# A two-layer encoder on one core: masks added by the row-maximum operation, the rotation's second stage a unit later, turns in three pieces of heads

## The chip, the cores and the metric

The kernel runs on one core of a Trainium2 chip. The metric is device time in microseconds (us) of one execution of the whole program; lower is better. The core's engines are PE (TensorE: matrix products and transposes), DVE (VectorE), ACT (ScalarE), POOL (GpSimd) and SP, which here issues DMAs. Each engine executes its own instructions strictly in the order in which they stand, and waits for others through semaphores. Matrix products write to PSUM banks, everything else lies in SBUF.

## The reference

Two groups of rows, a prompt of 256 and a sample of 512, go through two layers of width D = 1024. Each sub-layer is `x + post_norm(f(pre_norm(x)))`. Layer 0 mixes by windowed attention with sinks, layer 1 by differential attention; each is followed by a SwiGLU layer. Cut to the two mixers:

```python
# layer 0: 16 query heads of 64, 4 key/value heads, window 128
sc = jnp.where(valid, sc, -jnp.inf)                  # |q - k| <= 128, inside the sequence
m = jnp.maximum(jnp.max(sc, axis=-1, keepdims=True), sink)
e = jnp.exp(sc - m)
p = e / (jnp.sum(e, axis=-1, keepdims=True) + jnp.exp(sink - m))

# layer 1: 8 heads, each with two query/key parts of 64 and values of 128
q, k = apply_rope(q, cos, sin), apply_rope(k, cos, sin)
#   apply_rope: [x1 * c - x2 * s, x2 * c + x1 * s]
p = jax.nn.softmax(sc, axis=-1)
a = p[:, :, 0] - lam * p[:, :, 1]
o = rms_norm(a @ v, subln_g) * (1.0 - lambda_init)   # per head
```

## The kernel before

The 768 rows are six tiles of 128: tiles 0 and 1 the prompt, 2 to 5 the sample. Matrix products with weights are made in fp32 precision from three products of high and low parts, high x high, high x low, low x high (`product_steps`, L346 to L348). A tile framework places the instructions: the program's text gives the order in which they are issued, and each engine keeps its share of it, shifted only where the framework's scheduler sees an operand late.

**First mixer** (some 20 to 262 us of the trace). 24 units of 4 key/value heads x 6 tiles; each unit has four items, one for each query head. `score` makes an item's scores (sc, 128 x 256 or 128 x 384, L661 and L662), `normalize` divides by the sum, `turn_e` transposes the block (tpe, L697) for the value products (poa). `item(n)` puts in a row the scores of item n, the normalising of item n - 1 and the turn of item n - 3, and between the items stand the products with weights of a later unit (pqa), shared out evenly by `weave`. The mask of the window is added on PE: two constant bf16 blocks (`mask_l`, `mask_r`) are multiplied by a bf16 identity into the same PSUM bank (L664, L666), 64 times each. DVE then takes the row maximum (L668) and scales it against the sink (negm, L671); ACT makes the exponential out of PSUM with its sum (L677) and the sink's exponential (L679); DVE adds, inverts and scales (L686 to L688).

**Second mixer** (some 790 to 1115 us). The products with weights come in 50 units (`b_fill`): 32 for q and k by head and half of the rows (`rotated`), 18 for v. At the end of a q or k unit, `end` rotates: ACT copies the product out of PSUM (xq, xk), four DMAs on POOL's queue write a copy with the partitions swapped (L836), DVE multiplies x by the cosine (z, L838) and the swapped copy by the sine (L839), adds (L840), ACT casts the high part (qb, kb, L849), DVE subtracts for the low part (L852, L856). Scores and values of the attention (`score`, `turn_e`, `values`: bsc, be, tpa, aT, pob) are placed between the products by a table `events` of times in units; `placed` puts each at its fraction of its unit. Head h, tile t is score number 6h + t. After the 50 units a list `run` written by hand orders the rest (the tail): scores and values of the last heads, turns of the attention's output (tp_o, hhi, L438 and L445), and the first products with the output weights (po). `values` normalises groups of heads, 0 to 3, 4 to 6 and 7, with a reciprocal root that POOL computes (L390, L391) and multiplies in (L944). The turn of a tile is made in two pieces, heads 0 to 3 and 4 to 7.

The lines of the table of times, before:

```python
for h, start, stop in (
        (0, 12, 16.7), (1, 16.7, 22.2), (2, 22.2, 28.8), (3, 29.6, 34.8), (4, 34.8, 40.3), (5, 40.3, 46)):
    spread(h, start, stop)
events += [(47.9 + t / 2, "s", 6 * NT + t) for t in range(4)]
```

## Time and profile before

| | |
|---|---|
| time, median of 3 runs (smallest, largest) | 1678.19 us (1677.85, 1679.21) |
| the profiled execution: its own time, its span | 1678.24 us, 1676.5 us |
| busy: PE, DVE, ACT, POOL | 98%, 74%, 56%, 10% of the span |
| TensorE's clock granted in 140 to 180 us | 1.00 |

The profiled execution is as long as the median, so durations from its trace can be set against the runs without a correction. Times in the profile are microseconds from the span's start; a row of the timeline gives start, duration, engine, line, operation, tile written and tiles read, and in brackets how long the engine had been idle and what ended it. A group's row gives busy time in all and the mean of one in nanoseconds, then the idle time ahead of its instructions and what ended it. PE's products overlap, so what one costs is the distance to the start of the next. Line numbers are those of the kernel before; most of the same statements stand three lines higher after the change.

### The profile page before, as it was taken

What the parts mean: (1) busy time and instruction counts of PE and PEld (TensorE: products, weight loads), DVE (VectorE), ACT (ScalarE), POOL (GpSimd) and SP (SyncE); (2) the same over time, 40 slices, a digit from 0 to 9 for tenths busy, and PEclk for the clock granted to TensorE, in tenths of its full rate; (3) what the DMA queues carried; (4) which work ended last, traced back from release to release, by engine and by line L of the source; (5) the groups of instructions that cost most, each with busy time, mean ns of one, the idle gap of its engine ahead of it and who ended that gap; (6) DMA issues with size and microseconds to landing.
All of it is one profiled execution on the core that took longest, in us unless ns stands there. A gap on an engine that the chain in (4) does not pass through costs nothing. (4 is left out here: it accounts for less than half of the span.)

```text
span 1676.5 us, 25190 instructions
## 1 busy us (share of the span) xinstructions
PE 1638.5 (98%) x9291; PEld 1495.1 (89%) x9291; DVE 1235.2 (74%) x2210; ACT 943.9 (56%) x2080; POOL 162.5 (10%) x276
## 2 busy tenths in 40 slices
PE   7999999999999999999999999999899999999998
PEld 7888878899999998888999989877899999998886
DVE  7888776896766656988685775765897666666985
ACT  6777775654444444556566666675744444444653
POOL 1000001000000000001330451331000000000000
PEclk9999999999999999999999999999999999999999
DMA  5111014534233337675432322314434343337664
GB/s 214 39 39 47 15 39 148 179 131 143 101 127 108 129 125 246 225 268 192 127 84 61 76 71 75 104 31 139 166 119 147 104 142 109 129 115 242 237 244 156
DMA packets 68187, 217.53 MB, mean 130 GB/s; under 512 B 9248, under 2 KB 13472, under 8 KB 67808
## 3 DMA queue, kind: packets, MB, share of 16 engines
q1 hardware_dynamic: 54576, 175.93, 30.9%
q0 software_dynamic: 13344, 39.73, 8.1%
q8 instruction: 73, 1.20, 0.3%
q14 instruction: 50, 0.41, 0.1%
q10 hardware_dynamic: 144, 0.26, 0.0%
HBM read 163.59 MB, written 42.86 MB: 123 GB/s over the span
## 5 line engine op out<-in xcount | busy, mean ns | idle before, releaser
L254 DVE TENSOR_TENSOR wlo<-wraw,whi 128x1024 fp32r<-128x1024 f32 (+2 forms) x174 | 204.6, 1179 | 176.7 <-ACT whi L253 175.2
L253 ACT CAST whi<-wraw 128x1024 fp32r<-128x1024 f32 (+2 forms) x174 | 175.8, 1012 | 119.9 <-PE py L347 59.1
L346 PE MATMUL py<-hhi,whi 128*128 128x384 f32 x464 | 155.4, 335 | 0.9 <-ACT u L1029 0.9
L348 PE MATMUL py<-hhi,wlo 128*128 128x384 f32 x464 | 155.0, 334 | 0.0
L347 PE MATMUL py<-hlo,whi 128*128 128x384 f32 x464 | 155.0, 334 | 0.0
L334 ACT CAST hhi<-araw 128x768 fp32r<-128x768 f32 (+1 forms) x74 | 57.6, 783 | 88.7 <-DMA araw<-act 85.9
L348 PE MATMUL pv<-whi,hlo 128*128 128x512 f32 (+1 forms) x240 | 92.2, 384 | 0.4 <-DVE hlo L335 0.4
L346 PE MATMUL pv<-whi,hhi 128*128 128x512 f32 (+1 forms) x240 | 92.4, 385 | 0.0
L347 PE MATMUL pv<-wlo,hhi 128*128 128x512 f32 (+1 forms) x240 | 92.2, 384 | 0.0
L335 DVE TENSOR_TENSOR hlo<-araw,hhi 128x768 fp32r<-128x768 f32 (+1 forms) x74 | 65.3, 890 | 32.3 <-ACT hhi L334 32.2
L346 PEld LDWEIGHTS py<-hhi,whi 128*128 128x128 f32 x464 | 87.1, 188 | 1.8 <-ACT u L1029 1.5
L347 PEld LDWEIGHTS py<-hlo,whi 128*128 128x128 f32 x464 | 87.1, 188 | 0.0
L348 PEld LDWEIGHTS py<-hhi,wlo 128*128 128x128 f32 x464 | 87.1, 188 | 0.0
L346 PE MATMUL po<-whi,hhi 128*128 128x512 f32 x192 | 78.8, 410 | 3.3 <-ACT hhi L445 2.9
L1082 POOL DMA_DIRECT2D act<-st x22 | 19.4, 882 | 635.9 <-DVE st L1081 635.9
L347 PE MATMUL po<-wlo,hhi 128*128 128x512 f32 x192 | 75.4, 393 | 0.8 <-DVE wlo L254 0.8
L348 PE MATMUL po<-whi,hlo 128*128 128x512 f32 x192 | 76.0, 396 | 0.2 <-DVE hlo L335 0.2
L346 PE MATMUL pqa<-whi,hhi 128*128 128x384 f32 x192 | 73.7, 384 | 0.0
L346 PE MATMUL px<-hhi,whi 128*128 128x384 f32 x208 | 70.2, 339 | 2.7 <-ACT hhi L334 2.7
L898 ACT ACTIVATE be<-bsc,bmx 128x512 f32<-128x512 f32 (+1 forms) x96 | 58.5, 614 | 24.6 <-DVE bmx L896 24.3
L347 PE MATMUL px<-hlo,whi 128*128 128x384 f32 x208 | 70.0, 337 | 1.2 <-DVE hlo L335 1.2
L391 POOL TENSOR_TENSOR rstd_post<-rstd_post,mhalf 128x1 f32<-128x1 f32 x23 | 16.4, 716 | 557.9 <-ACT rstd_post L390 557.9
(315 smaller groups left out, 5112.9 us busy)
## 6 DMA issues: line engine op xcount, KB each, us to landing
act<-st POOLq DMA_DIRECT2D x22, 1344.0 KB, 6.6
wraw<-in_wgu SPq DMA_DIRECT2D x56, 512.0 KB, 4.6
araw<-act SPq DMA_DIRECT2D x70, 384.0 KB, 4.1
y_wraw<-in_wgu SPq DMA_DIRECT2D x40, 512.0 KB, 3.8
wraw<-in_wd SPq DMA_DIRECT2D x40, 512.0 KB, 4.0
xd<-x SPq DMA_DIRECT2D x18, 512.0 KB, 3.0
x<-xd SPq DMA_DIRECT2D x18, 512.0 KB, 3.9
wraw<-in_wo SPq DMA_DIRECT2D x16, 512.0 KB, 3.5
```

Source lines behind the costliest of these rows:

```text
L253: state["raw_hi"] = nc.scalar.copy(out=hi, in_=src)
L254: state["raw_lo"] = nc.vector.tensor_tensor(out=lo, in0=src, in1=hi.bitcast(F32), op=ALU.subtract)
L334: state["hi"] = nc.scalar.copy(out=hi, in_=src)
L335: state["lo"] = nc.vector.tensor_tensor(out=lo, in0=src, in1=hi.bitcast(F32), op=ALU.subtract)
L346: nc.tensor.matmul(out, ah, bh, start=start and i == 0, stop=False, skip_group_check=more)
L347: nc.tensor.matmul(out, ah, bl, start=False, stop=False, skip_group_check=more)
L348: nc.tensor.matmul(out, al, bh, start=False, stop=stop and i == last, skip_group_check=more)
L391: nc.gpsimd.tensor_tensor(out=r[:, :w], in0=r[:, :w], in1=mhalf[:, :w], op=ALU.pow)
L898: nc.scalar.activation(out=e[:, :n * P], in_=s, func=AF.Exp, bias=mx, accum_out=den[:, c:c + 1])
L1082: nc.gpsimd.dma_start(out=at_hand[c // 4][:, :, c // 2 % 2], in_=out.pop(c // 2))
```

## The change

First mixer: the two mask blocks become one fp32 block of 384 columns (left, zeros, right), in a pool that is closed after this mixer. One DVE instruction (`tensor_tensor_reduce`) adds the mask to the scores, multiplies by -1/8, writes the result to SBUF and takes its minimum with the negated sink into negm. The exponential reads that result with a scale of -1. Normalising goes by pairs of heads: every second item normalises the two before it, and the sink's exponential is made there for both.

Second mixer: `end` now stops after the multiplication by the cosine; the rest (`rest`: sine, sum, high and low parts, k's DMAs) is issued after the following unit, behind the instruction in `state["mark"]`. The table's times move by 0.2 to 0.8 units, the sixth head has three scores in it in place of four, and a new kind "o" turns heads 0 to 3 of tiles 0 to 2 at units 48.3 to 49.3. Turns come in three pieces (heads 0 to 3, 4 to 6, 7; `turn_heads`), and the hand-written tail is ordered anew with them.

```diff
+    mask = early.tile([P, 3 * P], F32, name="mask")
+    nc.gpsimd.memset(mask, 0.0)
+    for at, step, mult in ((0, 1, -1), (2 * P, -1, 1)):
         nc.gpsimd.affine_select(
-            out=m, in_=m, compare_op=ALU.is_ge, fill=MASK, base=0,
+            out=mask[:, at:at + P], in_=mask[:, at:at + P], compare_op=ALU.is_ge, fill=MASK, base=0,
             pattern=[[step, P]], channel_multiplier=mult,
...
-                left, right = k0 < t, k1 > t + 1
                 nc.tensor.matmul(s, q[i][:, j], kh[gi, first][:, keys], start=True, stop=False)
-                nc.tensor.matmul(s, q[i][:, j], kl[gi, first][:, keys], start=False, stop=not (left or right))
-                if left:
-                    nc.tensor.matmul(s[:, :P], ident_b, masks[0], start=False, stop=not right)
-                if right:
-                    nc.tensor.matmul(s[:, (nk - 1) * P:], ident_b, masks[1], start=False, stop=True)
-                mx = small.tile([P, 1], F32, tag="mx", name=f"mx{i}_{j}")
-                nc.vector.tensor_reduce(out=mx, in_=s, axis=AX.X, op=ALU.max)
+                nc.tensor.matmul(s, q[i][:, j], kl[gi, first][:, keys], start=False, stop=True)
                 h = gi * 4 + j
-                negm = small.tile([P, 1], F32, tag="negm", name=f"negm{i}_{j}")
-                nc.vector.tensor_scalar(
-                    out=negm, in0=mx, scalar1=-HD ** -0.5, scalar2=nsink[:, h:h + 1], op0=ALU.mult, op1=ALU.min)
                 if j % 2 == 0:
-                    e2[0] = new_y(f"e{i}_{j}")
-                e = e2[0][:, j % 2 * 512:j % 2 * 512 + nk * P]
-                den = small.tile([P, 2], F32, tag="den", name=f"den{i}_{j}")
-                nc.scalar.activation(
-                    out=e, in_=s, func=AF.Exp, bias=negm, scale=HD ** -0.5, accum_out=den[:, 0:1])
-                nc.scalar.activation(out=den[:, 1:2], in_=negm, func=AF.Exp, bias=sink[:, h:h + 1])
-                blocks[i, j] = e, den
-
-            e2 = {}
+                    pair[0] = (
+                        new_y(f"e{i}_{j}"), small.tile([P, 2], F32, tag="negm", name=f"negm{i}_{j}"),
+                        small.tile([P, 4], F32, tag="den", name=f"den{i}_{j}"))
+                e2, negm, den = pair[0]
+                e, c = e2[:, j % 2 * 512:j % 2 * 512 + nk * P], slice(j % 2, j % 2 + 1)
+                side = (k0 - t + 1) * P
+                nc.vector.tensor_tensor_reduce(
+                    out=e, in0=s, in1=mask[:, side:side + nk * P], scale=-HD ** -0.5, scalar=nsink[:, h:h + 1],
+                    op0=ALU.add, op1=ALU.min, accum_out=negm[:, c])
+                nc.scalar.activation(out=e, in_=e, func=AF.Exp, bias=negm[:, c], scale=-1.0, accum_out=den[:, c])
+                blocks[i, j] = e, den, negm
+
+            pair = {}
 
             def normalize(i, j):
-                e, den = blocks[i, j]
-                nc.vector.tensor_tensor(out=den[:, 0:1], in0=den[:, 0:1], in1=den[:, 1:2], op=ALU.add)
-                nc.vector.reciprocal(out=den[:, 0:1], in_=den[:, 0:1])
-                nc.vector.tensor_scalar(out=e, in0=e, scalar1=den[:, 0:1], scalar2=None, op0=ALU.mult)
+                h = (i // NT) * 4 + j
+                _, den, negm = blocks[i, j]
+                nc.vector.tensor_tensor(out=den[:, 2:4], in0=negm, in1=sink[:, h:h + 2], op=ALU.add)
+                nc.scalar.activation(out=den[:, 2:4], in_=den[:, 2:4], func=AF.Exp)
+                nc.vector.tensor_tensor(out=den[:, 0:2], in0=den[:, 0:2], in1=den[:, 2:4], op=ALU.add)
+                nc.vector.reciprocal(out=den[:, 0:2], in_=den[:, 0:2])
+                for c in range(2):
+                    e = blocks[i, j + c][0]
+                    nc.vector.tensor_scalar(out=e, in0=e, scalar1=den[:, c:c + 1], scalar2=None, op0=ALU.mult)
 
             eTs = {}
 
             def turn_e(i, j):
-                e, _ = blocks.pop((i, j))
+                e = blocks.pop((i, j))[0]
...
-                if 1 <= n <= n_items:
-                    normalize(*items[n - 1])
+                if n % 2 == 0 and 2 <= n <= n_items:
+                    normalize(*items[n - 2])
...
+                    state["z"] = nc.vector.tensor_tensor(out=z, in0=s, in1=tab[0][:, half], op=ALU.mult)
+
+                    def rest():
+                        nc.vector.tensor_tensor(out=r, in0=r, in1=tab[1][:, half], op=ALU.mult)
+                        nc.vector.tensor_tensor(out=z, in0=z, in1=r, op=ALU.add)
...
+                    state["mark"] = state["z"]
+                    waiting.append(rest)
...
+            def turn_heads(t, k0, k1):
+                half, at = t // 3, (t % 3) * P
+                n = k1 - k0
+
+                def step():
+                    tp = bank(f"tp_o1_{t}_{k0}")
+                    for j in range(n):
+                        nc.tensor.transpose(tp[:, j * P:(j + 1) * P], o[t][:, (k0 + j) * P:(k0 + j + 1) * P], ident)
+                    v = tp[:, :n * P].rearrange("p (k n) -> p k n", k=n)
+                    h4, l4 = (m[half][:, k0:k1, at:at + P] for m in (h_hi, h_lo))
+                    nc.scalar.activation(out=h4, in_=v, func=AF.Copy, scale=subl)
+                    nc.vector.scalar_tensor_tensor(
+                        out=l4, in0=v, scalar=subl, in1=h4.bitcast(F32), op0=ALU.mult, op1=ALU.subtract)
+
+                return step
...
-            turn_o = [transposes(o[t], t, f"o1_{t}", subl) for t in range(NT)]
+            turn_o = [[turn_heads(t, *hs) for hs in ((0, 4), (4, 7), (7, 8))] for t in range(NT)]
...
+            def turned(steps):
+                for s in steps:
+                    with tc.issue_after(state["mark"].ins):
+                        s()
...
-                    (0, 12, 16.7), (1, 16.7, 22.2), (2, 22.2, 28.8), (3, 29.6, 34.8), (4, 34.8, 40.3), (5, 40.3, 46)):
+                    (0, 12.7, 17), (1, 17, 22.5), (2, 22.5, 29.3), (3, 30.3, 35.1), (4, 35.1, 40.5), (5, 40.5, 46.3)):
                 spread(h, start, stop)
-            events += [(47.9 + t / 2, "s", 6 * NT + t) for t in range(4)]
+            events += [(48.7 + t / 2, "s", 6 * NT + t) for t in range(3)]
             for n in range(2, len(events)):
                 events.append((events[n][0], "t", n - 2))
-            for n in range(3, 6 * NT + 4):
+            for n in range(3, 6 * NT + 3):
                 events.append((events[n][0], "v", n - 3))
-            kinds = {"s": score, "t": turn_e, "v": values}
+            events += [(48.3 + t / 2, "o", t) for t in range(3)]
+            kinds = {"s": score, "t": turn_e, "v": values, "o": lambda t: turn_o[t][0]()}
...
+                late = waiting[:]
+                waiting.clear()
                 for s in placed(att, [int((at - i) * len(fill)) for at, _, _ in now], fill):
                     s()
+                turned(late)
...
-            run = S(6, 4) + early[0] + T(6, 2) + V(6, 1) + early[1] + out[0][:2] + S(6, 5) + T(6, 3) + V(6, 2) + out[0][2:4]
+            run = S(6, 3) + T(6, 1) + V(6, 0) + out[0][:2] + [lambda: turned(late)] + S(6, 4) + T(6, 2) + V(6, 1) + out[0][2:4]
+            run += O(5, 1) + out[2][7:] + V(7, 5) + O(3, 2)
```

In the first mixer DVE's order around unit 12 changes as follows (mx row maximum, negm the scaled one, den the sum, y_e the block of exponentials; qk15, sp15, r15 belong to a later unit's rotation; ISA is the new instruction and its read). Before:

```order
L668 TENSOR_REDUCE mx12_1_2205<-sc12_1_2201 128x1
L671 TENSOR_SCALAR negm12_1_2207<-mx12_1_2205,nsink_108 128x1
L627 TENSOR_TENSOR sp15_2164<-qk15_2157,sp15_2164 128x4x64
L629 TENSOR_TENSOR sp15_2164<-qk15_2157,sp15_2164 128x128
L668 TENSOR_REDUCE mx12_2_2229<-sc12_2_2225 128x1
L686 TENSOR_TENSOR den12_0_2185<-den12_0_2185 128x1
L671 TENSOR_SCALAR negm12_2_2231<-mx12_2_2229,nsink_108 128x1
L687 RECIPROCAL den12_0_2185<-den12_0_2185 128x1
L688 TENSOR_SCALAR y_e12_0_2184<-y_e12_0_2184,den12_0_2185 128x256
```

And after:

```order
L667 ISA y_e12_0_1919,negm12_0_1920<-sc12_1_1940,mask_91,nsink_107 128x256
L667 ISA negm12_0_1920 128x1
L678 TENSOR_TENSOR den12_0_1921<-negm12_0_1920,sink_106 128x2
L624 TENSOR_TENSOR sp15_1904<-qk15_1897,sp15_1904 128x4x64
L626 TENSOR_TENSOR sp15_1904<-qk15_1897,sp15_1904 128x128
L667 ISA y_e12_2_1958,negm12_2_1959<-sc12_2_1955,mask_91,nsink_107 128x256
L667 ISA negm12_2_1959 128x1
L680 TENSOR_TENSOR den12_0_1921<-den12_0_1921 128x2
L681 RECIPROCAL den12_0_1921<-den12_0_1921 128x2
L684 TENSOR_SCALAR y_e12_0_1919<-y_e12_0_1919,den12_0_1921 128x256 x2
```

The scaling of head 0 stood behind the sum of head 0 alone; now it stands behind that of heads 0 and 1, with an add ahead of the sink's exponential and the third head's operation and its read in between.

In the second mixer DVE's order around the rotation of k of head 3, second half (xk3_1, zk3_1), and q of head 4 (xq4, zq4) was this (bmx the row maximum of the scores, wlo a weight's low part):

```order
L838 TENSOR_TENSOR zk3_1_10187<-xk3_1_10181,rope0_8532 128x384
L838 TENSOR_TENSOR zq4_0_10228<-xq4_0_10222,rope0_8532 128x384
L839 TENSOR_TENSOR xk3_1_10181<-xk3_1_10181,rope1_8534 128x384
L840 TENSOR_TENSOR zk3_1_10187<-zk3_1_10187,xk3_1_10181 128x384
L896 TENSOR_REDUCE bmx18_0_10264<-bsc18_0_10258 128x1
L896 TENSOR_REDUCE bmx18_1_10267<-bsc18_1_10259 128x1
L856 TENSOR_TENSOR kb3_10109<-zk3_1_10187,kb3_10109 64x384 x2
L839 TENSOR_TENSOR xq4_0_10222<-xq4_0_10222,rope1_8534 128x384
```

And after, from the first cosine product of head 4 on:

```order
L836 TENSOR_TENSOR zq4_0_9708<-xq4_0_9702,rope0_8020 128x384
L839 TENSOR_TENSOR xk3_1_9626<-xk3_1_9626,rope1_8022 128x384
L840 TENSOR_TENSOR zk3_1_9632<-zk3_1_9632,xk3_1_9626 128x384
L856 TENSOR_TENSOR kb3_9636<-zk3_1_9632,kb3_9636 64x384 x2
L251 TENSOR_TENSOR wlo151_9744<-wraw127_9506,whi151_9743 128x768
L836 TENSOR_TENSOR zq4_1_9755<-xq4_1_9749,rope0_8020 128x384
L839 TENSOR_TENSOR xq4_0_9702<-xq4_0_9702,rope1_8022 128x384
L899 TENSOR_REDUCE bmx18_0_9779<-bsc18_0_9773 128x1
L840 TENSOR_TENSOR zq4_0_9708<-zq4_0_9708,xq4_0_9702 128x384
```

Between the cosine product of head 4's first half (zq4_0) and its sine product (xq4_0) now stands a whole unit's work, and the row maxima of score 18 stand among the operations of that rotation.

At the tail's end PE's order was this (pob the attention's values of a score, po the products with the output weights):

```order
L918 MATMUL tpa47_12270<-ident_81,be47_12184 128x128 x4
L931 MATMUL pob46_12277<-vb2_2_11008,aT46_12243 128x128
L931 MATMUL pob46_12277<-vb2_3_11069,aT46_12243 128x128
L931 MATMUL pob46_12277<-vb2_4_11130,aT46_12243 128x128
L931 MATMUL pob46_12277<-vb2_5_11215,aT46_12243 128x128
L346 MATMUL po1_0_1_11834<-whi161_11727,hhi0_111 128x512
L347 MATMUL po1_0_1_11834<-wlo161_11728,hhi0_111 128x512
```

Behind these stand four more of the same products, the turn tp_o1_3_1, six products, the values pob47, six products and the turn tp_o1_4_1. After:

```order
L950 MATMUL pob46_11805<-vb2_5_10703,aT46_11758 128x128
L921 MATMUL tp_o1_5_4_11817<-ident_81,ob5_8010 128x128 x3
L343 MATMUL po1_0_2_11302<-whi161_11154,hhi0_110 128x512
L344 MATMUL po1_0_2_11302<-wlo161_11155,hhi0_110 128x512
L345 MATMUL po1_0_2_11302<-whi161_11154,hlo0_112 128x512
L950 MATMUL pob47_11830<-vb2_2_10496,aT47_11803 128x128
L950 MATMUL pob47_11830<-vb2_3_10557,aT47_11803 128x128
L950 MATMUL pob47_11830<-vb2_4_10618,aT47_11803 128x128
L950 MATMUL pob47_11830<-vb2_5_10703,aT47_11803 128x128
L921 MATMUL tp_o1_3_7_11842<-ident_81,ob3_8008 128x128
L921 MATMUL tp_o1_4_7_11856<-ident_81,ob4_8009 128x128
```

The turns of head 7 for tiles 3 and 4 stand directly behind the last values, and three products stand between the two last groups of values where twelve stood. The first turn of all, tp_o1_0_0, which had four PE rows between it and the first po product (po1_0_0), now stands inside the products of q of head 7's second half, 79 rows ahead of that product.

75 lines of the change are left out of this document (36 added, 39 removed).

## The prediction

> **What bounds the kernel now.** I read the page first, then the list of what TensorE (PE) waited for, then the first and second mixer by window and by instruction. The page's first part gives the busy time of the engines over the span of 1676.5 us:
>
> ```profile
> PE 1638.5 (98%) x9291; PEld 1495.1 (89%) x9291; DVE 1235.2 (74%) x2210; ACT 943.9 (56%) x2080; POOL 162.5 (10%) x276
> ```
>
> PE is idle for 1676.5 - 1638.5 = 38.0 us in all, so an edit pays either by taking instructions off PE or by ending one of its few waits. The rows of the windows (busy time of PE, its weight load, DVE, ACT, POOL, each with its count; granted PE clock; DMA share; GB/s) say how it stands in the first mixer (140 to 180 us) and in the second mixer's tail (1073 to 1115 us); the other two are stretches within the second mixer:
>
> ```profile
> 140.00:180.00 40.00, 40.00 (x290) 34.45 (x290) 34.04 (x130) 32.43 (x116) 0.00 (x0) 1.00 0.16 50
> 1073.00:1115.00 42.00, 38.01 (x217) 29.79 (x216) 32.06 (x65) 33.44 (x102) 18.07 (x26) 0.96 0.30 91
> 1003.10:1006.50 3.40, 3.40 (x14) 3.20 (x14) 2.07 (x6) 2.76 (x9) 0.27 (x1) 0.50 0.32 58
> 1085.00:1088.40 3.40, 3.40 (x15) 3.01 (x13) 2.25 (x5) 2.58 (x9) 1.31 (x3) 0.50 0.93 311
> ```
>
> In the first mixer PE has no idle time at all, while DVE (34.04 of 40) and ACT (32.43 of 40) are close behind. In the tail PE loses 42.00 - 38.01 = 4.0 us, and some at a lower clock. PE's waits between 820 and 1115 us (who waits, for whom, us in total, how often, the longest) are these:
>
> ```profile
> PE tpa L918 <- ACT aT L920: 4.1, 1, 4.1
> PE po L346 <- ACT hhi L445: 2.9, 1, 2.9
> PE pob L931 <- ACT aT L920: 1.2, 2, 1.0
> PE tpa L918 <- DVE be L906: 0.7, 2, 0.4
> PE tp_o L438 <- ACT aT L920: 0.3, 1, 0.3
> ```
>
> They add up to 9.2 us. Two of them make most of it, and each is followed by one of the 3.40 us stretches at clock 0.50 quoted above, which does in 3.40 us what takes 1.70 at full clock: 1.7 us more for each. So the second mixer holds 9.2 + 3.4 = 12.6 us that could go, and the first mixer only what its PE instructions take.
>
> **First mixer: what leaves PE.** 128 mask products and their 128 weight loads go; no other PE work changes. Their rows, and two places in the order of time (start, duration, engine, line):
>
> ```profile
> L664 PE MATMUL sc<-mask_l,ident_b 128*128 128x128 bf16 x64 | 14.7, 230 | 0.0
> L666 PE MATMUL sc<-mask_r,ident_b 128*128 128x128 bf16 x64 | 14.4, 224 | 0.0
> 82.23 0.23 PE L664 MATMUL sc<-mask_l,ident_b 128*128 128x128 bf16 x1
> 82.30 0.39 PE L697 MATMUL tpe<-ident,y_e 128*128 128x128 f32 x2
> 157.79 0.23 PE L666 MATMUL sc<-mask_r,ident_b 128*128 128x128 bf16 x1
> 157.83 0.42 PE L346 MATMUL pqa<-whi,hhi 128*128 128x384 f32 x1
> ```
>
> The mean of 230 ns is from start to modelled end and overlaps the neighbours; what a product costs is the distance from its start to the next start. Here that is 82.30 - 82.23 = 0.07 us, and at 157.79 0.04 us. 128 x 0.07 = **9.0 us**. The low end is 128 x 0.04 = 5.1 us; for the high end I add to each 0.04 twice as much again for a following product that starts slower (0.12 us, 15.4 us in all). I take 0.07, since most masks are followed by a transpose or another mask.
>
> **First mixer: what comes onto DVE and ACT.** Of before and after I need the row maximum, the small operations and the exponentials:
>
> ```profile
> L668 DVE TENSOR_REDUCE mx<-sc 128x1 f32<-128x256 f32 x64 | 26.8, 420 | 5.9 <-PE sc L664 3.3 <-PE sc L666 1.9
> L671 DVE TENSOR_SCALAR negm<-mx,nsink 128x1 f32<-128x1 f32 x96 | 20.1, 210 | 0.2
> L686 DVE TENSOR_TENSOR den<-den 128x1 f32<-128x1 f32 x96 | 14.8, 154 | 11.7 <-ACT den L679 11.3
> L906 DVE SCALAR_TENSOR_TENSOR be<-be,rho 128x256 f32<-128x256 f32 x16 | 7.7, 484 | 0.5
> L677 ACT ACTIVATE y_e<-sc,negm 128x256 f32<-128x256 f32 x64 | 31.0, 484 | 1.6 <-DVE negm L671 1.1 <-DVE den L686 0.2
> L677 ACT ACTIVATION_READ_ACCUMULATOR y_e<-sc,negm 128x1 f32 x96 | 19.8, 206 | 0.0
> L679 ACT ACTIVATE den<-negm,sink 128x1 f32<-128x1 f32 x96 | 28.5, 296 | 0.0
> ```
>
> The new operation (add the mask, scale, minimum, write 128x256) is in no row of before. Nearest are L668, which reads the same bank (0.42), and L906, two tensor inputs and one written out (0.48). It also leaves a read of the accumulator; the only such read is ACT's, 0.21, and DVE's own one-column operations take 0.15 to 0.21. I take 0.45 + 0.16 = 0.61 us against 0.42 + 0.21 = 0.63 removed: even. Bounds: 0.42 + 0.06, a read half hidden, 0.48; and two passes, 2 x 0.42 + 0.21 = 1.05 us. Adds and reciprocals go from 96 each to 48 each on two columns, with 48 adds for the sink's exponent (192 become 144): 48 x 0.154 = 7 us less on DVE over some 240 us. On ACT 48 small exponentials go (48 x 0.296 = 14 us). The exponential now reads SBUF instead of PSUM; of ACT's copies the one from PSUM took 379 ns and the one from SBUF 408 ns for 256 columns:
>
> ```profile
> L701 ACT COPY eT<-tpe 128x256 f32<-128x256 f32 x64 | 23.7, 379 | 11.3 <-PE tpe L697 11.2
> L625 ACT CAST sp<-qk 128x256 fp32r<-128x256 f32 x24 | 9.8, 408 | 10.9 <-DVE qk L567 10.9
> ```
>
> So 96 x 0.029 = 2.8 us more against 14 less, under the 40 - 32.43 = 7.6 us that ACT has free in 40. [...]
>
> **First mixer: what becomes late.** Throughput is not the danger, order is. Now two heads are normalised together: the first head's scaling waits for the second's row maximum, the sink's exponential on ACT (96 become 48, but the DVE add ahead of it and behind it are new links), and the third head's row maximum that stands ahead of it on DVE. Unit 12 before shows how much PE has in hand:
>
> ```profile
> 141.72 0.42 DVE L668 TENSOR_REDUCE mx<-sc 128x1 f32<-128x256 f32 x1
> 142.50 0.35 DVE L688 TENSOR_SCALAR y_e<-y_e,den 128x256 f32<-128x256 f32 x1
> 143.13 0.39 PE L697 MATMUL tpe<-ident,y_e 128*128 128x128 f32 x2
> ```
>
> The first head is scaled at 142.85 and turned at 143.13: 0.28 us in hand. After, the third maximum starts at the same 141.72 and ends with its read at 142.33; then come the add (0.15), the reciprocal (taken like an add, 0.15) and the scaling (0.35), 142.98, and up to 143.25 if the sink's exponential, behind a full exponential (0.48) and its read on ACT, comes last. PE, which is 0.14 us earlier by two masks, would be at its transpose at 142.99 (143.13 - 0.14): a wait of 0 to 0.4 us with the semaphores between. In 11 of the 24 units the order on PE is as before; in the rest more weight products stand ahead of the turn. 11 x 0.27 = **+3 us**, from 0 to 24 x 0.33 = 8. First mixer: -9.0 + 3 = -6.0. Behind a late transpose come ACT's copy and the value products, which stand an item later and are covered by that item's products (0.42 each).
>
> **Second mixer, the rotation.** DVE's multiplication by the sine waits for the swap by DMA, and everything behind it on DVE and, through z, on ACT waits too. The worst case:
>
> ```profile
> 999.49 1.32 DVE L839 TENSOR_TENSOR xk<-xk,rope 128x384 f32<-128x384 f32 x1 [2.44 <-DMA xk<-xk]
> 1001.43 1.04 ACT L849 CAST kb<-zk 64x384 fp32r<-64x384 f32 x2 [4.77 <-DVE zk L840]
> 1002.50 0.37 ACT L920 COPY aT<-tpa 128x256 f32<-128x256 f32 x1
> 1002.93 0.79 PE L918 MATMUL tpa<-ident,be 128*128 128x128 f32 x3 [4.10 <-ACT aT L920]
> DVE xk L839 <- DMA xk<-xk: 19.6, 10, 4.7
> L839 DVE TENSOR_TENSOR xk<-xk,rope x16: 546/559/1317, 808.5 to 1089.7; 128x384 f32<-128x384 f32 x16
> DMA to landing us min/median/max: 1.7/1.8/5.3
> ```
>
> DVE stood 2.44 us for the swap, ACT 4.77 us in front of the cast with the attention's copy aT queued behind it, and PE 4.10 us for aT. The last two rows are this line's sixteen multiplications for k (the first at 808.5, the last at 1089.7) and the time of the swap's DMAs from issue to landing. Fifty units fill that stretch, 281 / 50 = 5.6 us each, so with the rest of the rotation issued a unit later the median swap (1.8) has long landed and the longest (5.3) just so. So the 4.1, both pob waits (1.2), and the clock (1.7) go: -7.0. The rest's operations now stand between other units' scores; I allow +0.8, two waits of 0.4 as for be (L906), from 0 to another 4.1 us. k's DMAs move with them on the same queue, and the attention's times are 0.3 to 0.8 units later, which leaves k as ready as it was.
>
> **Second mixer, the tail.** Here PE waited for the first turned half:
>
> ```profile
> 1079.81 1.04 ACT L849 CAST qb<-zq 64x384 fp32r<-64x384 f32 x2 [1.34 <-DVE zq L840]
> 1082.40 0.68 ACT L445 ACTIVATE hhi<-tp_o,subl 128x512 fp32r<-128x512 f32 x1
> 1083.12 0.50 PE L346 MATMUL po<-whi,hhi 128*128 128x512 f32 x1 [2.93 <-ACT hhi L445]
> ```
>
> Turned some 60 products ahead now, the first three tiles' heads 0 to 3 are ready long before their products: -2.9, with the small waits (0.7 + 0.3) and the clock's 1.7, -5.6. At the end the new order puts the last heads of tiles 3 and 4 directly behind the last values. Between the values (pob) of tile 4 and its turn stand 11 PE instructions (3 and 1 transposes, 3 products, 4 value products); 38.01 us over the window's 217 makes 0.175 each, 1.9 us. What head 7 needs from pob to being ready is seen here:
>
> ```profile
> 1113.61 0.37 ACT L935 ACTIVATE ob<-pob,rden 128x128 f32<-128x128 f32 x1 [0.31 <-PE pob L931]
> 1115.97 0.62 POOL L944 TENSOR_TENSOR ob<-ob,rstd_sub 128x128 f32<-128x128 f32 x1
> ```
>
> 1115.97 + 0.62 - 1113.61 = 3.0 us, so PE waits 1.1 to 1.5 us where nothing waited before: +1.5. ACT, 33.44 us of 42 busy, would be busy 33.4 of 36 without PE's gaps, so I allow +0.7 for waits behind it. Tail: -5.6 + 2.2 = -3.4, from 0 to -5.6.
>
> [...]
>
> **Sum.** -6.0 - 7.0 + 0.8 - 3.4 = -15.6 us against the profiled execution's 1678.24 us, which is the median of the runs (1678.19) within 0.05: **1662.5 us**.
>
> **The rivals.**
> 1. *The first mixer gives its gain back.* The paired chain makes PE wait 0.4 us in all 24 units (9.6 us). For it: 0.28 us in hand in unit 12 and DVE at 85%. Against: 13 units have other products ahead of the turn. Then 1678.2 - 0 - 6.2 - 3.4 = 1668.6 us. Chance 0.2.
> 2. *The second mixer gains nothing.* The waits for aT return behind other operations, since ACT in the tail is the nearest to full, 33.44 of 42. Against: the two long waits have the swap in their chains. Then 1678.2 - 6.0 = 1672 us. Chance 0.15.
> 3. *Slower.* The new operation takes two passes over its columns on DVE, 0.84 us, and a read. In the stretch 140 to 180 us there are five units, 20 items: 20 x 0.42 = 8.4 us more on DVE, whose free time there is 6.0, and the chain of the pair holds two such operations more. The scaling is then 0.84 + 0.56 = 1.4 us later in each unit, 24 x 1.4 = 33.6 us, less the 9.0 of the masks and the 9.6 of the second mixer: 1678.2 + 15 = 1693 us. It decides when the operation is longer than about 0.75 us (0.3 us more, twice in a unit's first pair, 24 units: 14.4 us, nearly the whole gain). For it: it is the one instruction with no row. Against: L906 has two inputs and an output in 0.48. Chance 0.07.
> The forecast itself has 0.55, the remaining 0.03 being something that none of these names.
>
> **How the numbers follow.** The forecast's own range is 1656 to 1668 (masks 5 to 15, waits 0 to 8). With the first two rivals it reaches to 1675; below, 1654 takes the masks at 0.12 and few waits. Slower stays outside. A measurement of this kernel tells about 0.2%, 3.4 us, from no change: faster means under 1674.8. Faster gets nearly all of the forecast and the first rival and two thirds of the second, 0.86; the same 0.06; slower 0.08.
>
> **What would show it.** Right: no bf16 products in the first mixer; the new operation at 0.42 to 0.5 us; PE's waits for scaled blocks under 5 us there; no wait for aT over 1.5 us and no stretch at half clock near 1003 and 1085 us; a wait of 1 to 2 us at the last heads' turn. Wrong: tpe waiting for DVE in every unit, or the operation over 0.75 us; clock rows of 0.50 in the second mixer; the tail's ACT over 95% with PE waiting for be or aT throughout.

## The result, and the profile after

The changed kernel takes **1663.51 us** (median of 4, 1662.38 to 1666.93) against 1678.70 us for the kernel before beside it; the ratio is 0.9911, with a 95% interval of 0.9893 to 0.9929. That is 15.2 us less. The forecast was 1662.5 us with a range of 1654 to 1675 (1656 to 1668 without the rivals), so the sum held. Its terms held less well than their sum, as the stretches show.

First the page's busy line of the changed kernel's profiled execution, which has a span of 1660.5 us (1676.5 before) and took 1662.38 us:

```profile
PE 1625.0 (98%) x9163; PEld 1489.4 (90%) x9163; DVE 1222.9 (74%) x2167; ACT 934.6 (56%) x2038; POOL 168.0 (10%) x275
```

PE has 128 instructions fewer, and 13.5 us less busy time: 1638.5 became 1625.0.

To see where the time went I use four landmarks on PE: the last start of a value product of the first mixer (poa), the first product of the feed-forward layer (px), the first q product of the second mixer (pqb) and the last k product of its units (pkb). In a tile's view each row gives line, operation, tiles, count, the shortest, median and longest duration in ns, and the first and last start in us. Before:

```profile
L711 PE MATMUL poa<-eT,va x224: 379/379/431, 47.8 to 252.4; 128*64 128x256 f32 x112
L346 PE MATMUL px<-hhi,whi x208: 334/334/669, 298.9 to 1499.8; 128*128 128x384 f32 x104
L346 PE MATMUL pqb<-hhi,whi x128: 333/334/419, 788.6 to 1068.7; 128*128 128x384 f32 x128
L348 PE MATMUL pkb<-hhi,wlo x128: 334/334/343, 794.0 to 1077.1; 128*128 128x384 f32 x128
```

After:

```profile
L707 PE MATMUL poa<-eT,va x224: 379/379/430, 48.5 to 247.0; 128*64 128x256 f32 x112
L343 PE MATMUL px<-hhi,whi x208: 334/334/443, 293.6 to 1483.9; 128*128 128x384 f32 x104
L343 PE MATMUL pqb<-hhi,whi x128: 333/334/428, 782.1 to 1053.1; 128*128 128x384 f32 x128
L345 PE MATMUL pkb<-hhi,wlo x128: 333/334/346, 787.5 to 1062.4; 128*128 128x384 f32 x128
```

The differences of these times, taken stretch by stretch, are the account of the change:

| stretch | before to after | forecast |
|---|---|---|
| first mixer, to 252.4 / 247.0 | -5.4 us | -6.0 |
| its output projection and the first feed-forward layer, to 788.6 / 782.1 | -1.1 | 0 |
| the second mixer's units, to 1077.1 / 1062.4 | -8.2 | -6.2 |
| tail and second feed-forward layer, to the end | -1.3 | -3.4 |
| span | -16.0 | -15.6 |

Two of the rows need a closer look. The first value product itself starts 0.7 us later in this execution than before (48.5 against 47.8 us), so from the first to the last value product the mixer is 6.1 us shorter (204.6 to 198.5). In the last row all of the 1.3 us lies between the last k product and the last product with the output weights (102.0 to 100.7 us); the second feed-forward layer is the same within 0.1 us.

What TensorE still waits for in the first mixer and its projection, first before, then after (who waits, for whom, us in total, how often, the longest):

```profile
PE tpe L697 <- DVE den L686: 0.2, 1, 0.2
PE po L348 <- DVE hlo L335: 0.2, 1, 0.2
```

```profile
PE tpe L693 <- DVE y_e L684: 1.9, 4, 0.7
PE po L345 <- DVE hlo L332: 0.9, 2, 0.7
PE po L343 <- ACT hhi L331: 0.6, 1, 0.6
PE poa L707 <- ACT eT L697: 0.2, 1, 0.2
```

Waits rose from 0.4 to 3.6 us, so the mask products took about 5.4 + 3.2 = 8.6 us with them (9.3 if counted from the first value product). In the second mixer and its tail PE has two waits after the change, and neither was there before:

```profile
PE tpa L937 <- DVE be L909: 2.8, 1, 2.8
PE tp_o L921 <- POOL ob L963: 1.3, 1, 1.3
```

The five rows of waits that the forecast wanted to remove are gone; a longer wait for a block be has come. The windows say where the clock went: the stretch in which the long wait stood before, and the tail:

```profile
1000.00:1040.00 40.00, 40.00 (x246) 37.06 (x245) 25.82 (x50) 26.64 (x72) 5.89 (x12) 1.00 0.28 81
1063.00:1105.00 42.00, 39.16 (x225) 30.98 (x225) 32.20 (x68) 33.99 (x105) 17.60 (x24) 0.96 0.23 73
1072.80:1076.10 3.30, 3.18 (x14) 3.11 (x15) 3.25 (x7) 2.46 (x7) 1.61 (x3) 0.50 0.50 153
```

From 1000 to 1040 us PE is busy throughout at full clock, where before it stood 4.10 us and ran at 0.50 for another 3.40. In the tail it still loses 2.8 us and a stretch at half clock, which now follows the new wait. That wait is seen in the timeline of DVE and PE (start, duration, engine, line, operation):

```profile
1067.64 0.68 DVE L899 TENSOR_REDUCE bmx<-bsc 128x1 f32<-128x512 f32 x1
1068.35 1.65 DVE L852 TENSOR_TENSOR qb<-zq,qb 64x384 fp32r<-64x384 f32 x2
1069.93 0.68 DVE L899 TENSOR_REDUCE bmx<-bsc 128x1 f32<-128x512 f32 x1
1072.04 0.74 DVE L909 SCALAR_TENSOR_TENSOR be<-be,rho 128x512 f32<-128x512 f32 x1
1072.92 1.08 PE L937 MATMUL tpa<-ident,be 128*128 128x128 f32 x4 [2.84 <-DVE be L909]
```

The two subtractions for the low part of the last q (L852, 1.65 us) stand between the two row maxima of one score. This is the second stage of the rotation, moved a unit later, and now in the way of the scores behind which it was put. (How much of the wait hangs on that, the experiments on the tail show.)

The new operation itself, its read and the exponential out of SBUF, in the groups of the first mixer (busy us, mean ns):

```profile
L667 DVE CUSTOM_DVE_ANT_0 y_e<-sc,mask,nsink 128x256 f32<-128x256 f32 x64 | 30.6, 479 | 9.6 <-PE sc L658 8.9
L667 DVE DVE_READ_ACCUMULATOR2_ANT negm<- 128x1 f32 x96 | 7.9, 83 | 0.0
L670 ACT ACTIVATE y_e<-y_e,negm 128x256 f32<-128x256 f32 x64 | 32.9, 516 | 6.6 <-DVE negm L667 6.6
```

### The profile page after: what moved, and what is told of

Its sections match the earlier page's. It is cut to its first block, busy times and chain, and to the rows that moved or that the text cites. A ratio compares the mean times of both kernels' runs of the same rounds, so it can differ in the third digit from the quotient of the medians.

```text
span 1660.5 us, 24800 instructions
## 1 busy us (share of the span) xinstructions
PE 1625.0 (98%) x9163; PEld 1489.4 (90%) x9163; DVE 1222.9 (74%) x2167; ACT 934.6 (56%) x2038; POOL 168.0 (10%) x275
## 5 line engine op out<-in xcount | busy, mean ns | idle before, releaser
L388 POOL TENSOR_TENSOR rstd_post<-rstd_post,mhalf 128x1 f32<-128x1 f32 x23 | 19.8, 864 | 544.6 <-ACT rstd_post L387 544.6
L901 ACT ACTIVATE be<-bsc,bmx 128x512 f32<-128x512 f32 (+1 forms) x96 | 58.7, 616 | 20.0 <-DVE bmx L899 19.6
```

The costliest lines, as they stand in the source:

```text
L388: nc.gpsimd.tensor_tensor(out=r[:, :w], in0=r[:, :w], in1=mhalf[:, :w], op=ALU.pow)
L901: nc.scalar.activation(out=e[:, :n * P], in_=s, func=AF.Exp, bias=mx, accum_out=den[:, c:c + 1])
```

## The experiments

The questions were three: whether the two mixers' edits act apart and what each is worth; whether the pairing of heads is what costs the 3 us of waits in the first mixer; and whether the tail's new wait is the delayed rotation's doing. Times are medians; each ratio is to the kernel before on the same chip. The changed kernel itself was timed again only beside `q_late` and the three edits together; elsewhere the ratios are the fairer comparison with it.

### The first mixer's edit alone

On the kernel before, the parts of the diff up to the first mixer's end (mask, `score`, `normalize`, `item`, the early pool), the second mixer untouched; its core:

```diff
-                if left:
-                    nc.tensor.matmul(s[:, :P], ident_b, masks[0], start=False, stop=not right)
...
+                nc.vector.tensor_tensor_reduce(
+                    out=e, in0=s, in1=mask[:, side:side + nk * P], scale=-HD ** -0.5, ...)
...
-                if 1 <= n <= n_items:
-                    normalize(*items[n - 1])
+                if n % 2 == 0 and 2 <= n <= n_items:
+                    normalize(*items[n - 2])
```

> The kernel before with the first mixer's edit alone (mask added by the row-maximum operation, heads normalised in pairs). Theory: the two mixers do not touch each other, so this gives what the trace of the changed kernel shows for the first mixer, 242.7 to 237.2 us, -5.4: about 1673 us, with PE waiting about 3 us more there and the second mixer's waits of 4.1 and 2.9 us still in place. Rival: part of the second mixer's gain comes from the first edit (a transfer or a clock stretch that moved, the pool closed early): then over 8 us.

Measured: 1669.32 us against 1679.48, ratio 0.9935 (0.9919 to 0.9951), so 10.2 us less. In its trace the first mixer has the waits of the changed kernel and one more of 1.1 us, and its last value product starts at 248.0, 4.4 us earlier than before (from the first value product to the last it is 6.0 us shorter; the first starts 1.6 later here). The second mixer was not as before either:

```profile
PE po L343 <- ACT hhi L442: 2.9, 1, 2.9
PE tpa L915 <- ACT aT L917: 2.3, 1, 2.3
```

The wait for aT is 2.3 us in place of 4.1, though the program there is the same. So the expectation that the second mixer's waits stay as they were fell, and the rival's bound of 8 us was passed. Whether the first edit did this, or one execution differs so from another, a single trace of each cannot tell. The profiled spans differ by 7.3 us, of which the trace puts 4.4 at the end of the mixer and 2.4 in the units of the second. The rest of the 10.2 lies between executions: the profiled one took 1670.96 us, 1.6 above its median, and the one before 1678.24, 1.2 under the median of 1679.48 here.

### The rotation's delay alone

```diff
+                    waiting.append(rest)        # second stage, issued after the next unit
...
+                turned(late)
...
-  early[1] + out[0][:2] + S(6, 5)
+  early[1] + out[0][:2] + [lambda: turned(late_k)] + S(6, 5)
```

> The kernel before with the rotation's second stage a unit later and nothing else (the table of times, the turns and the tail as before; only the last unit's second stage is put into the tail, behind its first two steps of output products). Theory: this takes the 4.1 us wait for aT and its half-clock stretch, about 6 to 7 us, and leaves the tail's wait for the first turned half, so about 1672 us. Rival: the table and the turns are needed as well, the delayed operations only move the stall behind the scores, and the gain is under 3 us.

Measured: 1671.42 us, ratio 0.9948 (0.9935 to 0.9961), 8.1 us less. The wait for aT is gone and so is most of the wait for the first turned half, since q's casts no longer stand in front of it on ACT. The longest waits of the second mixer that are left:

```profile
PE tpa L924 <- DVE be L912: 0.8, 1, 0.8
PE po L346 <- ACT hhi L445: 0.7, 1, 0.7
```

DVE's waits for k's swap went from 19.6 us in 10 to

```profile
DVE xk L842 <- DMA xk<-xk: 1.4, 2, 1.2
```

The mechanism of the forecast holds, and it reaches further: the 2.9 us wait needed no earlier turn.

### The changed kernel without the delay

```diff
-                    waiting.append(rest)
+                    rest()
```

> The changed kernel with the rotation's second stage back at the end of its own unit; table, turns, tail and the first mixer stay changed. Theory: the wait for aT near the middle of the second mixer comes back with its clock stretch, and the tail loses its new 2.8 us wait for be, because the last q's second stage no longer stands among the last scores: about 1666 to 1669 us. Rival: the gain of the second mixer is that of the turns and the table, and the time stays within 2 us of 1663.5.

Measured: 1664.29 us, ratio 0.9911 (0.9896 to 0.9926), the ratio of the changed kernel. The rival was right. DVE waits for the swap again, and ACT behind it,

```profile
DVE xk L839 <- DMA xk<-xk: 8.5, 5, 3.1
ACT kb L849 <- DVE zk L840: 12.8, 7, 4.4
```

but TensorE does not wait in the units at all; its longest waits in the second mixer are in the tail:

```profile
PE tpa L937 <- ACT be L901: 1.9, 1, 1.9
PE bsc L893 <- ACT be L901: 1.2, 1, 1.2
```

So with the new times and turns the delay is worth nothing, although alone it is worth 8 us. The tail is no shorter without it either. The 2.84 us wait is gone (the mean granted clock of the execution is 0.998 in both), but beside the two waits above there are two more for be, 1.1 us together, and from the last k product to the last output product it takes 101.0 us, against 100.7 in the changed kernel.

### The new times alone

```diff
-  (0, 12, 16.7), (1, 16.7, 22.2), (2, 22.2, 28.8), (3, 29.6, 34.8), (4, 34.8, 40.3), (5, 40.3, 46)
+  (0, 12.7, 17), (1, 17, 22.5), (2, 22.5, 29.3), (3, 30.3, 35.1), (4, 35.1, 40.5), (5, 40.5, 46.3)
```

> The kernel before with the new times of the attention of heads 0 to 5 and nothing else (rotation, turns, tail, head 6 and the first mixer as before). Theory, formed after the first four runs: the 4.1 us wait comes from the DMAs of k's swap for head 5 standing interleaved with the normalising of heads 0 to 3 on POOL's queue; the new times put them apart, as in the changed kernel without the delay. Then the second mixer's units lose their 5.4 us of waits and a clock stretch, about 6 us, while the tail keeps its 2.9 us wait for the first turned half: about 1673 us. Rival: it was the early turns that took the wait away; then the wait for aT stays and the time is within 2 us of before.

Measured: 1672.22 us against 1678.49, ratio 0.9963 (0.9949 to 0.9976), 6.3 us less. As expected, no wait for aT is left and the 2.8 us wait for the first turned half stays:

```profile
PE po L346 <- ACT hhi L445: 2.8, 1, 2.8
```

The cause was told too narrowly. In the trace of before, POOL's queue has the four DMAs of the swap with k's own two (kb) and the normalising of heads 0 to 3 among them:

```profile
988.74 0.50 POOL L836 DMA_DIRECT2D xk<-xk  x1 [0.36 <-ACT xk L834]
992.90 1.16 POOL L391 TENSOR_TENSOR rstd_sub<-rstd_sub,mhalf 128x4 f32<-128x4 f32 x1
994.03 0.56 POOL L836 DMA_DIRECT2D xk<-xk  x1
994.62 1.05 POOL L944 TENSOR_TENSOR ob<-ob,rstd_sub 128x512 f32<-128x512 f32 x1
997.73 0.50 POOL L836 DMA_DIRECT2D xk<-xk  x1 [1.57 <-issue]
```

The last is issued 9.0 us behind the first. With the new times the four stand together and it is 4.3 us, though the last still comes late; nothing that the profile shows holds POOL up ahead of it:

```profile
991.44 1.49 POOL L836 DMA_DIRECT2D xk<-xk  x3
995.72 0.50 POOL L836 DMA_DIRECT2D xk<-xk  x1 [2.79 <-issue]
DVE xk L839 <- DMA xk<-xk: 12.0, 7, 3.2
```

So DVE goes on waiting up to 3.2 us for it. What the new times do is to put the copy aT where that wait no longer holds TensorE up. That the queue's mixture makes the swap longer is seen; that it is the whole cause is not shown. The profiled execution took 1675.99 us, the slowest of its five and 3.8 above their median; its units of the second mixer are 7.4 us shorter than before (288.5 to 281.1), and it loses time again in the first feed-forward layer, which the edit does not touch (last section).

### The new operation twice

```diff
                 nc.vector.tensor_tensor_reduce(
                     out=e, in0=s, in1=mask[:, side:side + nk * P], scale=-HD ** -0.5, ...)
+                nc.vector.tensor_tensor_reduce(
+                    out=e, in0=s, in1=mask[:, side:side + nk * P], scale=-HD ** -0.5, ...)
```

> The changed kernel with the new DVE operation issued twice for each item (same inputs, same result): 0.48 us and a read of 0.08 more, 96 times. It prices the third rival. By the order of the pair (two such operations stand in the chain of each unit's first pair) the time rises by 24 x 1.1 = 27 us to about 1690. By throughput alone DVE has 40 - 32.2 = 7.8 us free in 40, five units ask 20 x 0.56 = 11.2, so 3.4 in 40 or 20 us come on top: about 1683. If both are wrong and the rise is under 10 us, the operation's length was never near to deciding.

Measured: 1680.61 us, ratio 1.0004 (0.9992 to 1.0015): 17 us more than the changed kernel, and no gain left over before. In the trace 16.2 us of this lie between the first and the last value product of the first mixer (198.5 to 214.7). PE waits for scaled blocks in 17 places,

```profile
PE tpe L696 <- DVE y_e L687: 14.6, 17, 2.2
```

and the windows from 140 to 180 us, of the changed kernel and of this one, show DVE fuller and PE with gaps:

```profile
140.00:180.00 40.00, 39.55 (x269) 34.46 (x268) 32.19 (x118) 29.77 (x103) 0.00 (x0) 1.00 0.15 50
```

```profile
140.00:180.00 40.00, 36.84 (x238) 31.06 (x238) 34.67 (x138) 27.11 (x93) 0.00 (x0) 0.96 0.14 50
```

The price is nearest to the throughput count (20 us) and under the chain's count (27). That does not make throughput the cause: DVE is busy for 34.67 of the 40 us and not full, while PE waits for its blocks in 17 places. These waits grew by 12.7 us (14.6 - 1.9), most of the 16.2. This fits the chain better, with fewer units waiting than the 24 counted; that DVE's throughput has no part in it is not shown. Had the operation taken 0.56 us more, the whole change would have been worth nothing.

### Each head normalised for itself

```diff
-                if n % 2 == 0 and 2 <= n <= n_items:
-                    normalize(*items[n - 2])
+                if 1 <= n <= n_items:
+                    normalize(*items[n - 1])
```

with the add, the reciprocal and the scaling for one head, and the sink's exponential behind each head's own.

> The changed kernel with each head normalised for itself, an item after its scores as before, and the sink's exponential behind each head's exponential; the mask stays in the new operation. Theory: the pairing makes the four waits of TensorE for scaled blocks (1.9 us), so these go, while ACT (about 12 us more in the first mixer) and DVE (about 7 us more) still fit: 1.5 us faster than the changed kernel, about 1662. Rival: DVE and ACT are close enough to full that the 96 small exponentials and 96 small DVE operations more cost more than the waits, 1665 to 1668.

Measured: 1661.28 us, ratio 0.9889 (0.9874 to 0.9904). The waits for scaled blocks are gone, and of the others from the mixer's units and projection one of 0.4 us is left; ACT is fuller by 3.7 us in 40 and it does not matter:

```profile
PE po L345 <- DVE hlo L332: 0.4, 1, 0.4
140.00:180.00 40.00, 39.96 (x272) 35.64 (x272) 33.91 (x131) 33.43 (x118) 0.00 (x0) 1.00 0.15 50
L705 PE MATMUL poa<-eT,va x224: 379/379/431, 47.2 to 243.2; 128*64 128x256 f32 x112
```

The last value product starts at 243.2 us, 3.8 earlier than in the changed kernel and 9.2 earlier than before. Part of this is an earlier start: from the first value product to the last it is 196.0 us, against 198.5 and 204.6, so 2.5 and 8.6 less. So the pairing made the waits that took back a part of the masks' gain, and what it saved on ACT and DVE was not scarce. The medians differ by 2.2 us with intervals that overlap a little; the stretch is the clearer evidence.

### The tail: both second stages later, q's alone later, the last turns later

In the first, the second stages of the last q and k are issued behind scores 4 and 5 of head 6 (counted from 0, so 5 is its last); the loop over the units leaves the last q's out for that:

```diff
-                turned(late)
-            late = waiting[:]
+                if i < 49:
+                    turned(late)
+            late_q, late = late, waiting[:]
...
-  V(6, 0) + out[0][:2] + [lambda: turned(late)] + S(6, 4) + T(6, 2) + V(6, 1) + out[0][2:4]
+  V(6, 0) + out[0][:2] + S(6, 4) + T(6, 2) + V(6, 1) + [lambda: turned(late_q)] + out[0][2:4]
-  S(6, 5) + T(6, 3) + V(6, 2) + out[1][:2] + S(7, 0)
+  S(6, 5) + T(6, 3) + V(6, 2) + [lambda: turned(late)] + out[1][:2] + S(7, 0)
```

> The changed kernel with the second stages of the last two rotations (q and k of head 7, second half) put later in the tail: behind the fourth and fifth score of head 6. Theory: the new 2.84 us wait for be stems from q's second stage standing among the row maxima of the last scores on DVE; it goes, and with it the half-clock stretch where there is one: 2.8 to 4.5 us faster than the changed kernel, about 1660. Rival: the tail's exponentials on ACT are the limit and the wait appears at the next transposes: within 1 us of 1663.5.

Measured: 1664.51 us, ratio 0.9911 (0.9898 to 0.9925): no gain. The wait for be shrank to 0.4 us, but k now came too late for its scores, and a longer wait took its place:

```profile
PE bsc L893 <- DMA kb<-kb: 3.6, 1, 3.6
PE tpa L937 <- DVE be L909: 0.4, 1, 0.4
```

The later issue is not all of it: the two DMAs of this kb, issued at 1079.4 and 1080.0 us, took 5.4 and 5.6 us to land, where in the changed kernel they took 2.8 to 2.9. Why, the profile does not show.

The second adds, in the output projection,

```diff
-            if turn_o is not None and t + 1 < NT:
-                for s in turn_o(t + 1):
-                    s()
-            for s in out_unit(t, wk, o, 0, gp, sq, f"po{layer}_0_{t}"):
-                s()
+            turn = turn_o(t + 1) if turn_o is not None and t + 1 < NT else []
+            steps = out_unit(t, wk, o, 0, gp, sq, f"po{layer}_0_{t}")
+            for s in steps[:4] + turn + steps[4:]:
+                s()
```

> As the run before, and in the output projection the turn of the next tile's head 7 stands behind four of the eight steps of a tile's products in place of ahead of them. Theory: the wait of 1.3 us for the normalised head 7 of tile 4 goes, with nothing in its place: 1.3 us faster than the run before, about 1659. Rival: the later turn makes the next tile's products wait for its high and low parts (about 1.4 us of conversion) and nothing is won.

Measured: 1665.10 us, ratio 0.9908 (0.9893 to 0.9922), with runs from 1660.56 to 1665.54. The 1.3 us wait for the last normalised head is no longer among PE's waits and nothing stands in its place, as expected; the wait for kb is 3.3 us. The time does not tell it from the run before; in the traces the stretch from the last k product to the last output product is 2.1 us shorter (102.3 to 100.2).

The third leaves k's second stage where the change has it and moves q's alone, behind the last score of head 6:

```diff
-  S(6, 5) + T(6, 3) + V(6, 2) + out[1][:2] + S(7, 0)
+  S(6, 5) + T(6, 3) + V(6, 2) + [lambda: turned(late_q)] + out[1][:2] + S(7, 0)
```

> The changed kernel with the second stage of the last q rotation alone put behind the last score of head 6; k's stays where the change has it. Theory: of the two rotations in the tail q's is the one that held up the row maxima; without it there the 2.84 us wait for be goes, and k's DMAs are not late as in the two runs before (waits of 3.6 and 3.3 us for kb): 2 to 3 us less in the tail than the changed kernel, about 1661. Rival: the tail is bound by ACT and DVE anyway, a wait of the same size appears at a transpose or at a score within the next 10 us.

Measured: 1660.72 us, ratio 0.9885 (0.987 to 0.99), beside 1663.65 for the changed kernel. The wait of 2.84 us is gone. In its place stands one of 1.7 us, now for an exponential on ACT, with another of 0.7 for a low part on DVE, and the tail has no stretch at half clock:

```profile
PE tpa L937 <- ACT be L901: 1.7, 1, 1.7
1063.00:1105.00 42.00, 39.51 (x235) 30.89 (x234) 32.18 (x68) 34.86 (x110) 18.67 (x25) 1.00 0.22 73
```

PE's busy time in the window grew only from 39.16 to 39.51 of 42: most of the wait moved, as the rival said; the time came from the clock, 0.96 to 1.00 over 42 us, 1.7 us. The stretch from the last k product to the last output product agrees, 99.2 us against 100.8 in the changed kernel beside it; the rest of the 2.9 us between the medians is not in the tail.

### The three edits together, and the changed kernel again

Each head normalised for itself, the last q later, and the turn in the projection later, by the three diffs above (`normalize(*items[n - 1])`, `turned(late_q)` behind the last score of head 6, `steps[:4] + turn + steps[4:]`). The second kernel is the changed kernel with no edit.

> The changed kernel with three edits together: each head normalised for itself, the last q's second stage later, and the next tile's turn of head 7 behind four of the eight steps of a tile's products. Theory: the parts lie in different stretches and add up: -2.2 measured for the first, about -2.5 for the second, -1.3 for the third: 1657 to 1658 us. Rival: as with the rotation's delay and the new times, two of them cure the same stall; then 1660.

> The changed kernel itself, beside these two on the same chip: 1663.5 us by every theory. It shows how far the same program's stretches move from one execution to the next, above all the first feed-forward stretch, which was 488.5 to 494.4 us in the runs so far though no edit touches it.

Measured: the three together 1657.76 us, ratio 0.9864 (0.9847 to 0.988); the changed kernel beside it 1663.65 us, ratio 0.9904 (0.989 to 0.9919). The intervals lie apart: 5.9 us less than the changed kernel, 22.6 less than the kernel before. That is the sum that was expected, though the third part was never timed alone. In the traces the first mixer is 2.3 us shorter than in the changed kernel beside it (from the first value product to the last) and the tail 3.3 us shorter (97.5 against 100.8 us), which makes 5.6. Two executions of the changed kernel, the one of the result and this one, have the second mixer's units equal at 280.3 us, the tail at 100.7 and 100.8, and the first feed-forward stretch at 488.5 and 490.0.

## Why the prediction was right, point by point

**What bounds it.** Right in the stretches examined. PE was the bound there (before, busy for all of the 40 us from 140 to 180), and the time moved with PE's instructions and PE's waits; DVE and ACT, busy for 85% and 81% of the same time, cost only where an order made PE wait.

**The masks, -9.0.** Right. The first mixer without paired waits ends 9.2 us earlier and is 8.6 us shorter from the first value product to the last; the distance from start to start (0.07 us), not the duration (0.23 us), was the price. By the duration it would have been 29 us.

**The new operation at 0.61 us with its read.** Right, 0.479 + 0.083 = 0.56 for 256 columns. One of the two halves was off: DVE's read of its accumulator takes 0.08 where ACT's took 0.21.

**The exponential from SBUF, +0.029 us.** Right: 516 - 484 = 32 ns. ACT had the room: from 140 to 180 us it was busy for 32.43 of the 40 us before and for 29.77 after.

**What becomes late, +3.** Right in cause, since the waits go when each head is normalised for itself; that the size came out too (3.2 us) is in part luck. The path that the prediction named, the scaled blocks, made 1.9 us, and not as 0.27 in 11 units but as four waits of up to 0.7. Another 1.5 us are waits for the projection's high and low parts, which the prediction did not name; of these 0.4 are left without the pairing.

**The second mixer's units, -6.2.** The long wait, the waits for aT and the stretch at half clock went. The measured -8.2 is larger. I allowed 0.8 for new waits where none came, and one score of head 6 left the units for the tail while the turns of three tiles came in. But "the rest of the rotation a unit later" was not what was needed: the new times alone take the wait away too, and in the changed kernel the delay adds nothing. The number was right by a cause that is enough alone (8.1 us by itself) but that the changed kernel does not need. The prediction put the whole gain down to the delay and looked at the new times only for whether k was ready.

**The tail, -3.4.** This is the term that failed: -1.3. The two rows that it named came out (the wait for the turned half gone, a new one of 1.3 where 1.5 was forecast). The 0.7 that I allowed "for waits behind ACT" was mis-sized: what came was a wait of 2.84 us for DVE, with the delayed second stage of the last q among the row maxima, and with it a half-clock stretch of the kind that I had counted as gone, 1.7 us. A clock row of 0.50 in the second mixer was one of the prediction's own signs of being wrong. The engine is not the whole story: with q's stage out of the way (`q_late`) a wait of 1.7 us for ACT stands there, and without the delay (`no_delay`) the tail is as long. A little came back: two waits for parts of the output weights, 0.8 and 0.2 us near 1147 us, went too, behind the 1115 us at which the prediction's list of waits ended. The sum came out because the rest was made up by the units and by the 1.1 us in the feed-forward layer, which is luck.

**The feed-forward layer, 0.** The 1.1 us there come with a stretch at half clock near 300 us, which the profile of before had and this one has not, though PE waits 1.4 us for ACT ahead of it in both. Whether the change has a part in it is open. The longest px product of 384 columns (334 ns in the median) took 689 ns in that profile of before and 445 in this one; it took 445 or 446 in three others with heads normalised in pairs (`a_only`, `no_delay`, `ttr_twice`) and 686 to 689 in four with each head normalised for itself (`rot_only`, `table_only`, `single_norm`, `best`), and these rows do not say in which of the two feed-forward layers.

**The rivals.** The first (the chain gives all back) did not come, 3.2 us in place of 9.6. The second came in a small way: a wait for be in the tail in place of the one removed. The third needs a longer operation than I said: doubling it cost 17 us for 0.56 us, so if the price is even it would decide at about 0.5 us more, not at 0.3. Its 1.4 us in each unit has a term of 0.56 that the prediction does not explain; measured were 16.2 us in the mixer, 0.7 in each unit.

**Small slips.** The sum -15.6 from 1678.2 is 1662.6, not 1662.5. The 281 us by which a unit's length was found run from the first sine product of a k to the last; the units' own stretch is 288.5 us, so 5.8 each, not 5.6. Neither changes the argument.

## What to carry to other kernels

Price what leaves a full engine by the distance to the next start (0.07 us here, where the duration was 0.23), and then look for the instruction whose operand the new order makes late: here the pairing of two heads paid back a third of the gain, and undoing it was free because the engines that it relieved had room (DVE 33.91 and ACT 33.43 of 40 us busy without it). A stall of the bound engine can have several cures, each sufficient alone, as the wait for aT had here (8.1 and 6.3 us less, each edit by itself); do one alone and leave one out before crediting any of them. Work that is moved out of the way can land in front of something else, as the last q's second stage did (1.65 us on DVE, a wait of 2.84 us on PE), so find the place where the last piece of it comes down; here no later unit covered it.

## What the runs showed of the hardware

**The clock after a wait.** Between TensorE's first product and its last, the two profiles of the result have three single waits of 2.8 us or longer, and a stretch of 3.4 us at clock 0.50 starts near the end of each, from 0.1 us ahead of it to 1.9 us behind it. Before, the waits of 4.10 and 2.93 us ended at 1002.93 and 1083.12 us, and the stretches run from 1003.1 to 1006.5 and from 1085.0 to 1088.4; after, the wait of 2.84 us ended at 1072.92, and the stretch runs from 1072.8 to 1076.2. The run with the operation doubled has a wait of 2.9 us in the tail and a window at 1.00:

```profile
PE tpa L940 <- DVE be L912: 2.9, 1, 2.9
1080.00:1120.00 40.00, 37.13 (x224) 29.00 (x224) 31.39 (x68) 33.62 (x104) 16.86 (x23) 1.00 0.25 79
```

The other runs have seven more waits of 2.8 to 3.6 us; what the clock did behind those is not shown here. Of the shorter ones, one of 2.3 us for aT, with the first mixer's edit alone, has a row of 0.56 from 996.0 to 999.4 us beside it, and behind one of 1.4 us, in the profile of before, the clock was 0.51 from 299.9 to 303.3 us. Others had no such stretch: the profile after has waits of 2.0, 1.4 and 1.3 us and a clock of 1.00 from 10 to 1072 and from 1077 to 1654 us, and in the tail `q_late` has one of 1.7 us and the three edits together one of 1.6 us, both with 1.00 from 1063 to 1105 us. What sets the two kinds apart is not shown. So of the four waits of 2.8 us or longer whose clock is shown, three cost 1.7 us beside themselves (3.4 us at half clock for what takes 1.7 at full), and shorter ones sometimes did. The prediction's allowance of 0.7 us for new waits in the tail had no clock in it.

**How far an untouched stretch moves.** Between the first px and the first pqb no edit of this study changes an instruction. In the profiles that stretch took 782.1 - 293.6 = 488.5 us in the changed kernel and 494.4 us with the new times alone:

```profile
L346 PE MATMUL px<-hhi,whi x208: 334/334/667, 298.4 to 1497.6; 128*128 128x384 f32 x104
L346 PE MATMUL pqb<-hhi,whi x128: 333/334/421, 792.8 to 1065.6; 128*128 128x384 f32 x128
```

In the second, PE has a wait of 3.4 us there for the next layer's input, which the first has not; its longest px product took 687 ns against 445 in the first, and its mean granted clock over the whole execution is 0.994 against 0.998. The two executions of the changed kernel differ by 1.5 us in this stretch (488.5 and 490.0). Six us between two profiles are as large as several of the effects here, so comparing stretches tells more than comparing totals.
